# A batched matrix product on one core: the store of group 1 cut into three transfers of 112, 15 and 1 partitions

## The chip, the cores and the metric

The kernel runs on one core of a Trainium2 chip. A core has a matrix engine (TensorE, PE), three other compute engines (VectorE or DVE, ScalarE or ACT, GpSimd or POOL), an engine that issues transfers (SyncE, SP) and 16 DMA engines, which move data between the chip's memory (HBM) and the core's on-chip memory (SBUF, 128 partitions). The metric is the device time of one execution in microseconds. Before the change its median is 132.35 us over 3 runs (132.32 to 132.53).

## The reference

```python
def setup_inputs():
    batch, dim_i, dim_j, dim_k = 32, 256, 512, 384
    return {
        "x": np.random.randn(batch, dim_i, dim_j).astype(np.float32),
        "y": np.random.randn(batch, dim_j, dim_k).astype(np.float32),
    }

def reference(x, y):
    return np.einsum('bij,bjk->bik', x, y).astype(np.float32)
```

There are 32 independent products of a 256 x 512 matrix with a 512 x 384 matrix, in 32-bit floats. x is 16.8 MB, y 25.2 MB and the output 12.6 MB.

## The kernel before, in words

The 32 products are taken in N = 8 groups of Q = 4. For each group the kernel loads a tile of x and a tile of y (two buffers of each, used in turn), casts both to 16 bits on GpSimd, transposes x on VectorE, multiplies on TensorE, copies the results out of PSUM with ScalarE and VectorE, and stores them.

The 128 partitions are four blocks of 32, one for each product of the group. In the output, partition p of group n holds eight consecutive rows of 384 numbers, so one partition's part is 12,288 bytes that lie together both in SBUF and in HBM. The output tile `o_sb` has a slot of its own for each of the 8 groups: a store never makes a later group wait for a buffer.

All transfers are issued by SP, in an order written out by hand. First come the loads of groups 0 and 1, ahead of the main program. Then a loop at the head of SP's part issues the loads of groups 2 to 7 (`load_x` on line 70, `load_y` on line 74), each after a wait for GpSimd's casts of the buffer that it fills. Only then comes a second loop over n from 0 to 7, which issues the stores through `store(n)` (line 97). Ahead of each store stands a wait: for n below 7 until TensorE has finished the first chunk of the second half of group n + 1, which it starts only after group n has been copied out; for n = 7 for the last copies themselves. So in SP's order every load stands ahead of every store.

Each transfer adds 16 to a semaphore when it has landed. The stores share one, `s_out`; nobody looks at it but SP's last instruction (line 112), which waits for 16 x 8 = 128 and takes the count back to zero. That wait is the end of the kernel. POOL clears the other semaphores once SP has issued all stores.

TensorE, VectorE, ScalarE and GpSimd have programs of their own, bound by semaphores; the change touches none of them.

Of the kernel before, what the change touches and what calls it, by code (L numbers as in the profile page):

```python
# [10 lines left out]
P = 128  # L11
Q = 4
NE = 2
STEP = 4
PIECES = 4


@with_exitstack
def kernel(
# [16 lines left out]
    N = B // Q  # L36
    NC = T // STEP
    TY = T // PIECES

# [23 lines left out]
    s_out = nc.alloc_semaphore("s_out")  # L63
# [25 lines left out]
    def chunk_done(n, e, a):  # L89
        return (n * NE + e) * MARKS + (a + 1 if a < NC - 1 else MARKS)  # L90

    sp = nc.sync

    def store(n):
        dst = out[n * Q : (n + 1) * Q].rearrange("g (s f) k -> (g s) f k", s=PQ)
        src = o_sb[:, n].rearrange("p e h k -> p (e h) k")
        sp.dma_start(out=dst, in_=src).then_inc(s_out, 16)

    for n in range(2, N):
        sp.wait_ge(s_cast, NE * (n - 1))  # L100
# [3 lines left out]
    for n in range(N):  # L104
        if n < N - 1:
            sp.wait_ge(s_pe, chunk_done(n + 1, NE - 1, 0))
        else:
            sp.wait_ge(s_act, NE)
            sp.wait_ge(s_dve, NE)
        store(n)  # L110
    sp.sem_inc(s_sp, 1)
    sp.wait_op(s_out, 16 * N, "sem-ge").then_inc(s_out, -16 * N)


    po = nc.gpsimd
    for n in range(N):
# [9 lines left out]
        po.wait_ge(s_y[n], 16)  # L126
        for a in range(PIECES):
            if n:
                po.wait_ge(s_pe, chunk_done(n - 1, NE - 1, (a + 1) * NC // PIECES - 1))
            s = slice(a * TY, (a + 1) * TY)  # L130
            ins = po.tensor_copy(y_r[:, s], y_sb[n % 2][:, s])  # L131
            ins.then_inc(s_yr, 1 if a < PIECES - 1 else 1 + PIECES)
    po.wait_ge(s_sp, 1)
# [124 lines left out]
```

## Time and profile before

| | |
|---|---|
| median of 3 runs | 132.35 us (132.32 to 132.53) |
| the profiled execution | 132.6 us |
| its span | 131.3 us |
| moved by DMA | 54.54 MB (41.94 read from HBM, 12.58 written) |
| DMA transfers | 8 of x (2048 KB each), 8 of y (3072 KB), 8 stores (1536 KB) |
| mean granted TensorE clock | 0.845 |

The profile is of one execution, and its span is the time between the first and the last instruction. Busy times are for each engine over the span; the DMA share is the mean over the core's 16 DMA engines, counted at the start of each packet, which is why a short stretch can show a little over 1. A packet is one piece that one DMA engine moves. In a list of instructions, `L97` is line 97, `SPq` is SP's queue, and "x8" means eight of them. "To landing" is the time from the issue of a transfer until its last byte has been counted on the semaphore. A wait row reads: who waited, at which line, for whom; total us, number of times, longest. A row of the table of stretches reads: from, to, length, busy time (and number of instructions) of PE, PE's weight loads, DVE, ACT and POOL, then the granted clock, the DMA share and the GB/s.

### The profile page before, as it was taken

What the parts mean: (1) busy time and instruction counts of PE and PEld (TensorE: products, weight loads), DVE (VectorE), ACT (ScalarE), POOL (GpSimd) and SP (SyncE); (2) the same over time, 40 slices, a digit from 0 to 9 for tenths busy, and PEclk for the clock granted to TensorE, in tenths of its full rate; (3) what the DMA queues carried; (4) which work ended last, traced back from release to release, by engine and by line L of the source; (5) the groups of instructions that cost most, each with busy time, mean ns of one, the idle gap of its engine ahead of it and who ended that gap; (6) DMA issues with size and microseconds to landing.
All of it is one profiled execution on the core that took longest, in us unless ns stands there. A gap on an engine that the chain in (4) does not pass through costs nothing. (4 is left out here: it accounts for less than half of the span.)

```text
span 131.3 us, 3324 instructions
## 1 busy us (share of the span) xinstructions
PE 64.7 (49%) x1024; PEld 44.1 (34%) x1024; DVE 73.7 (56%) x128; ACT 91.6 (70%) x194; POOL 75.8 (58%) x52
## 2 busy tenths in 40 slices
PE   0000059907980967467278808961994497200000
PEld 0000057606750944235165504441873354100000
DVE  0006005885499499758956993699359859600000
ACT  0400000999599999999997999699969999996000
POOL 0037195589957974997399549857955960000000
PEclk9999999995599599999968997797569869995555
DMA  5999999999999999999999999999999999999994
GB/s 105 419 459 427 417 424 457 427 419 429 457 402 429 437 449 392 439 452 434 402 449 434 424 407 452 442 399 434 449 434 389 429 419 427 438 427 423 431 431 202
DMA packets 3458, 54.54 MB, mean 415 GB/s; under 512 B 384, under 2 KB 384, under 8 KB 384
## 3 DMA queue, kind: packets, MB, share of 16 engines
q1 hardware_dynamic: 3456, 54.53, 97.9%
q14 instruction: 2, 0.02, 0.0%
HBM read 41.94 MB, written 12.58 MB: 415 GB/s over the span
## 5 line engine op out<-in xcount | busy, mean ns | idle before, releaser
L149 ACT COPY o_sb<-o_ps x192 | 90.2, 470 | 24.9 <-PE o_ps L193 22.6
L193 PE MATMUL o_ps<-y_r,xt_sb 32*128 32x384 f16 x1024 | 64.7, 387 | 47.9 <-PEq L190 42.0
L193 PEld LDWEIGHTS o_ps<-y_r,xt_sb 32*128 32x128 f16 x1024 | 44.1, 106 | 68.0 <-issue 58.8
L145 DVE STREAM_TRANSPOSE xt_sb<-x_r 128x256 f32<-128x256 f32 x64 | 38.1, 624 | 38.7 <-PE o_ps L193 27.1
L131 POOL CAST y_r<-y_sb 128x1536 f16<-128x1536 f32 x32 | 45.6, 1467 | 14.0 <-DMA y_sb<-in_y_dram 13.8
L121 POOL CAST x_r<-x_sb 128x2048 f16<-128x2048 f32 x16 | 30.3, 1893 | 17.3 <-DVE o_sb L149 8.8
L149 DVE COPY o_sb<-o_ps 32x384 f32 (+1 forms) x64 | 35.6, 556 | 2.5 <-PE o_ps L193 1.1
L179 ACT ACT_TABLE_LOAD x1 | 1.3, 1283 | 3.7 <-PEq L79 3.7
L242 POOL MEMSET const-float32-0.0<- 128x1 f32 x1 | 0.1, 98 | 0.2 <-issue 0.2
L179 ACT COPY spare<-const-float32-0.0 1x1 f32<-1x1 f32 x1 | 0.2, 190 | 0.0
L242 POOL MEMSET const-bfloat16-1.0<- 128x1 bf16 x1 | 0.1, 101 | 0.0
L242 POOL MEMSET const-uint8-127<- 128x1 uint8 x1 | 0.1, 101 | 0.0
L242 POOL MEMSET const-float32-1.0<- 128x1 f32 x1 | 0.1, 98 | 0.0
## 6 DMA issues: line engine op xcount, KB each, us to landing
y_sb<-in_y_dram SPq DMA_DIRECT2D x8, 3072.0 KB, 16.8
x_sb<-in_x_dram SPq DMA_DIRECT2D x8, 2048.0 KB, 19.0
out_dram<-o_sb SPq DMA_DIRECT2D x8, 1536.0 KB, 24.5
```

Source lines behind the costliest of these rows:

```text
L121: po.tensor_copy(x_r[:, e], x_sb[n % 2][:, e * H : (e + 1) * H]).then_inc(s_cast, 1)
L131: ins = po.tensor_copy(y_r[:, s], y_sb[n % 2][:, s])
L145: v.transpose(xt_w[:, w], words[:, e, w]).then_inc(s_xt, 1)
L149: ins = copy(o_sb[g * PQ : (g + 1) * PQ, n, e, h], o_ps[h * PQ : (h + 1) * PQ, e * Q + g, :K],)
L179: a_.copy(spare, nc.const_aps.tensor(0.0, [1, 1], F32))
L193: return te.add_instruction(mybir.InstMatmult(name=nc.get_next_instruction_name(), start_tensor_calc=start, stop_tensor_calc=stop, tile_si ...
L242: nc = _bacc.Bacc("TRN2", target_bir_lowering=False, num_devices=1)
```

## The change

`store(1)` issues three transfers where it issued one: partitions 0 to 111, then 112 to 126, then 127. The other stores go as one transfer, as before. Each transfer adds 16 to `s_out`, so SP's last wait asks for 16 x 10 = 160.

```diff
+PARTS = [112, 15, 1]
...
     def store(n):
         dst = out[n * Q : (n + 1) * Q].rearrange("g (s f) k -> (g s) f k", s=PQ)
         src = o_sb[:, n].rearrange("p e h k -> p (e h) k")
-        sp.dma_start(out=dst, in_=src).then_inc(s_out, 16)
+        p = 0
+        for w in PARTS if n == 1 else [P]:
+            sp.dma_start(out=dst[p : p + w], in_=src[p : p + w]).then_inc(s_out, 16)
+            p += w
...
-    sp.wait_op(s_out, 16 * N, "sem-ge").then_inc(s_out, -16 * N)
+    sp.wait_op(s_out, 16 * (N + len(PARTS) - 1), "sem-ge").then_inc(s_out, -16 * (N + len(PARTS) - 1))
```

## The prediction

> **What bounds the kernel now.** I read four views, in this order: the head of the page (how busy each engine is), the table of stretches (which resource is full in which stage), the waits of the issuing queue SP, and the packets of the last microseconds. First the page.
>
> ```profile
> span 131.3 us, 3324 instructions
> PE 64.7 (49%) x1024; PEld 44.1 (34%) x1024; DVE 73.7 (56%) x128; ACT 91.6 (70%) x194; POOL 75.8 (58%) x52
> ...
> DMA packets 3458, 54.54 MB, mean 415 GB/s; under 512 B 384, under 2 KB 384, under 8 KB 384
> ...
> q1 hardware_dynamic: 3456, 54.53, 97.9%
> ```
>
> No compute engine is busy for more than 70% of the span; the 16 DMA engines together are busy for 97.9% of it. The packets also tell how a transfer is cut. The kernel issues 24 transfers, and 384 small packets are 24 x 16, so each transfer ends with one small completion write on each of 16 engines. The other 3072 are 24 x 128: one packet per partition row. A row of a store is 1536 KB / 128 = 12 KB, and each engine carries 8 of them.
>
> The table of stretches (length, then busy time of five engines, clock, DMA share, GB/s) says when this holds:
>
> ```profile
> 13.00:26.00 13.00, 8.03 (x127) 6.17 (x128) 4.78 (x8) 2.83 (x7) 7.34 (x5) 1.00 1.01 434
> 26.00:85.00 59.00, 37.27 (x592) 24.61 (x587) 43.83 (x76) 54.03 (x116) 47.40 (x31) 0.86 1.01 431
> 85.00:104.00 19.00, 11.73 (x193) 8.75 (x184) 15.32 (x28) 17.54 (x38) 13.73 (x9) 0.82 0.99 424
> 104.00:128.50 24.50, 7.64 (x127) 4.62 (x125) 7.58 (x13) 15.77 (x34) 3.30 (x3) 0.71 1.01 428
> 128.50:131.30 2.80, 0.00 (x0) 0.00 (x0) 0.00 (x0) 0.00 (x0) 0.00 (x0) 0.50 0.37 158
> ```
>
> The DMA share is full from 13 us to 128.5 us, so what is put on the DMA engines is paid for at the end. The stores run behind the last loads, at 428 GB/s: 1536 KB (1.573 MB) / 428 GB/s = 3.67 us for a store, and with 8 rows for each engine 0.458 us for a row.
>
> Next the stores themselves, in the answer for the output tensor, and SP's own waits:
>
> ```profile
> L97 SPq DMA_DIRECT2D out_dram<-o_sb x8: 332/430/437, 85.1 to 120.2; - x8
> DMA to landing us min/median/max: 11.0/24.5/33.2
> ...
> SPq L97 <- PE o_ps L193: 24.0, 5, 12.2
> SPq L112 <- SPq L112: 10.7, 1, 10.7
> SPq L97 <- ACT o_sb L149: 5.3, 1, 5.3
> ```
>
> A store lands 11.0 to 33.2 us after its issue, though it needs 3.67 us of the engines. The last, issued at 120.2, lands at 120.2 + 11.0 = 131.2, which is the span: three stores lie in the queue even then. SP waits for compute (24.0 and 5.3 us in all) and it costs nothing, since the DMA engines have their backlog. SP's last wait, 10.7 us, is for the stores to land, and it ends the kernel.
>
> Last, the packets from 129 us on, in 40 slices of 0.0575 us. One 12 KB row starting in a slice shows as 12,288 B / 0.0575 us = 214 GB/s, two as 427:
>
> ```profile
> GB/s 641 214 0 427 214 214 427 214 427 0 0 0 0 0 427 214 0 0 0 0 0 0 214 0 0 0 0 0 0 0 0 0 0 0 0 0 0 0 0 0
> DMA packets 33, 0.21 MB, mean 91 GB/s; under 512 B 16, under 2 KB 16, under 8 KB 16
> ...
> 129.70:130.00 0.30, 0.00 (x0) 0.00 (x0) 0.00 (x0) 0.00 (x0) 0.00 (x0) 0.50 0.29 123
> 130.00:130.25 0.25, 0.00 (x0) 0.00 (x0) 0.00 (x0) 0.00 (x0) 0.00 (x0) 0.50 0.00 0
> 130.25:130.30 0.05, 0.00 (x0) 0.00 (x0) 0.00 (x0) 0.00 (x0) 0.00 (x0) 0.50 0.01 0
> 130.30:131.30 1.00, 0.00 (x0) 0.00 (x0) 0.00 (x0) 0.00 (x0) 0.00 (x0) 0.50 0.03 12
> ```
>
> The engines do not end together. Three rows start at about 129.8 to 129.9, and then one engine alone starts a last row at about 130.3. It runs 0.03 x 16 x 1.00 = 0.48 us, the same as a row among sixteen, and lands 0.9 us after it began. Call this the late engine: it has no slack, the next ones have about 0.4 us, the rest up to a microsecond. The rows do not say which of the sixteen it is.
>
> **The change part by part.** It removes one transfer of 128 rows and adds three, of 112, 15 and 1 rows, at the same place in SP's order. The bytes are the same.
>
> Issue on SP: two more issues at 0.332 to 0.437 us each, at most 0.87 us. They stand between store 1 and store 2. Stores 2 to 7 come up to 0.87 us later to a queue that holds 11.0 us of work at its emptiest, and SP itself waits 24.0 us for PE behind them. Cost 0; if the backlog were gone, 0.87 us. The waits in front of the stores are unchanged and no wait is added. The last one asks for 160 in place of 128, with nothing behind it on SP but the end. PE, ACT, DVE and POOL wait for no store, since every group has its own slot of the output tile: 0.
>
> Completion writes: with three transfers an engine makes up to two more. One such write stands alone in the stretch 130.25 to 130.30: 0.01 x 16 x 0.05 = 0.008 us. Two are 0.02 us.
>
> The 112 rows: 112 / 16 = 7 for each engine, if all sixteen share. At the row time that is 3.21 us, and with one more row each it would be the 3.67 of before. No transfer in the trace has fewer than 128 partitions, so whether its rows go at 0.458 us is not shown. In the whole transfer each engine has eight partitions to itself; cut into sevens the shares lie across those eights, and two engines can come to read from the same eight. Bounds: 0, if partitions may be read from any engine at full pace; 7 rows (3.2 us), if every engine shares its path with another all along. The nearest row is the whole transfer, which has 8 row times where this has 7; I take one row, 0.46 us.
>
> The 15 rows: one each for 15 engines, and none for one. The rows are neighbours. Bounds: one row time and no loss, if each engine reads at its own pace as the lone row at 130.3 did; and 15 row times, 6.9 us and so 14 rows lost, if fifteen neighbours come through one path of that same 27 GB/s (428 / 16). The ends are far apart. I take the geometric middle of 1 and 15, four rows in succession, so three rows lost: 1.37 us. It is nearer to the no-loss end, because a lone engine and an engine among sixteen have the same pace and the trace shows no loss in company.
> [...]
>
> The one row: 1/16 row for each engine (0.03 us) if the 12 KB are cut into sixteen; a whole row (0.46) if they stay one packet on the late engine, or if the sixteen parts leave the same partition one after another. I take the row, 0.46, since in every transfer shown a row is one packet.
> [...]
>
> Sum: 1 + 3 + 1 = 5 rows of 0.458 us = 2.29 us, plus 0.02, on an engine without slack. Later stores cannot give it back, for the share is 1.01 until 128.5. The profiled execution took 132.6 us, 1.3 more than its span, and is 0.25 above the median of 132.35. On its span: 133.6. On the median: 132.35 + 2.3 = 134.7. Both ends of all parts: -0.46 (a row less on the late engine) to 22 rows, 10 us.
>
> **The rivals.** *Nothing to see.* Any engine reads any partition at full pace, and the last row is cut sixteen ways or falls to an engine with slack. Then the late engine has 0.02 us of completion writes and 0.03 of the cut row: 132.4. For it: the lone row's pace and the steady 424 to 434 GB/s whatever is moved. Against: all that steadiness is of 128-row transfers.
>
> *Faster: the late engine is the one that the 15 rows leave out.* Then it does 7 rows for store 1 in place of 8, and its last row starts 0.46 us earlier. The engines next to it, 0.4 us ahead, set the end then: 132.35 - 0.4 = 131.95. It decides only if that engine is the late one (1 of 16 if all are alike) and if sharing costs it less than 0.46 us. For it: exactly one late row in the tail. Against: the odds, and any shared path.
>
> *One engine carries the single row whole.* No sharing, but the late engine does 9 rows: 132.35 + 0.46 = 132.8. It decides only if it falls on that engine; on others it is within 0.4 us of slack and vanishes into the first rival.
>
> *Worse sharing.* The 112 rows are dealt out singly, so that sixteen neighbours are read at one time all through: up to the 22 rows of the bounds, 137.2 to 142.4.
>
> **How the numbers follow.** A difference under 0.2% (0.26 us) is about what a measurement of this kernel cannot tell from none. Chances: sharing that costs 0.6 to 4.9 us, with 134.7 as its likeliest, 0.68; worse sharing 0.10; nothing to see 0.12; faster 0.08; one engine alone 0.02. Sharing has most of it because the bounds run from 0 to 22 rows and already the loss of one row on a late engine without slack counts as slower; only at no sharing at all does the time stay. Slower is 0.68 + 0.10 + 0.02 = 0.80, same 0.12, faster 0.08. The range begins just under no change, 132.3, and leaves out the faster case (0.08). It ends at twice the five rows, 4.6 us, plus the 0.25 by which profile and median differ: 137.2. That leaves out the worse sharing (0.10). The slower case alone reaches from 133.0 to 137.2.
>
> **What would show it.** In the changed kernel the packets say how the last row went: 3502 on the hardware queue if it was cut into sixteen (3456 - 144, + 128, + 30, + 32), 3472 if it stayed one (+ 2 in place of + 32). If sharing is right, the GB/s fall under 400 for a few slices where store 1 moves, about 105 to 109 us, while the DMA share stays at 1.0, for the rows take longer; the last store lands over 12 us after its issue; PE, ACT and DVE end where they did. If nothing is shared, the GB/s keep to 424 or more there, and the tail ends again with one lone row near 130.3. If the late engine was left out, the tail has no lone row and ends near 130.8. The prediction is wrong above all if four neighbours go as fast as sixteen strangers, or if the late engine comes to the shared path after the others have gone and pays for none of it.

## The result and the profile after

The changed kernel takes 133.46 us (median of 4 runs, 133.15 to 133.75), the kernel before 132.43 us on the same chip: a ratio of 1.0078, 95% interval [1.0064, 1.0092]. It is slower, by 1.03 us [0.85, 1.22]; 2.3 us were forecast. The direction and the range held, the size did not. A run over 1.5% above the fastest of its kernel counts in no ratio: that leaves out, of the experiments below, two of the eight runs with partitions 0 to 111 alone (134.2 us) and one of the four with all eight stores cut (147.05 us).

From the page of the changed kernel, the lines that answer to those of before:

```profile
span 132.3 us, 3326 instructions
PE 65.3 (49%) x1024; PEld 44.5 (34%) x1024; DVE 73.7 (56%) x128; ACT 91.8 (69%) x194; POOL 75.8 (57%) x52
...
GB/s 114 431 446 439 399 451 416 461 401 471 387 426 436 463 409 421 421 461 424 409 444 431 421 416 451 431 416 426 468 394 416 419 364 424 427 420 431 439 431 141
DMA packets 3474, 54.54 MB, mean 412 GB/s; under 512 B 400, under 2 KB 400, under 8 KB 400
...
q1 hardware_dynamic: 3472, 54.53, 97.6%
...
out_dram<-o_sb SPq DMA_DIRECT2D x7, 1536.0 KB
out_dram<-o_sb SPq DMA_DIRECT2D x1, 1344.0 KB
out_dram<-o_sb SPq DMA_DIRECT2D x1, 180.0 KB
out_dram<-o_sb SPq DMA_DIRECT2D x1, 12.0 KB
```

The compute engines are as busy as before and the bytes are the same. There are 3472 packets on the hardware queue: the last row stayed one packet of 12 KB on one engine, and the small packets, the completion writes, went from 384 to 400 (16 + 15 + 1 for store 1 where there were 16). One slice of the GB/s row, from 105.8 to 109.1 us (number 33), is far below its neighbours: 364. That is where store 1 moves.

The table of stretches of the changed kernel (length, busy times, clock, DMA share, GB/s):

```profile
26.00:85.00 59.00, 38.53 (x596) 24.55 (x595) 44.23 (x77) 54.27 (x116) 47.15 (x30) 0.83 1.01 430
85.00:104.00 19.00, 11.52 (x192) 8.75 (x185) 15.20 (x28) 17.41 (x38) 14.01 (x9) 0.81 1.00 426
104.00:112.00 8.00, 7.05 (x126) 5.27 (x118) 5.08 (x9) 7.79 (x18) 3.01 (x3) 0.81 1.01 396
128.50:132.30 3.80, 0.00 (x0) 0.00 (x0) 0.00 (x0) 0.00 (x0) 0.00 (x0) 0.50 0.41 175
```

and the stretch of store 1 before:

```profile
104.00:112.00 8.00, 7.09 (x122) 4.50 (x124) 5.35 (x9) 7.79 (x17) 3.30 (x3) 0.79 1.01 427
```

Up to 104 us the rates are those of before (430 and 426 against 431 and 424). In the eight microseconds with store 1, the DMA engines are as busy (share 1.01) and move 396 GB/s in place of 427. A share of 31 / 427 of 8 us is lost: 0.58 us, as a mean over the engines. The single packets show how. A row takes 0.460 us in the median in both kernels. Over 0.6 us before there is one row (0.915 us). After there are these twelve, by start, duration and end in ns:

```
104923 1182 106105
104994  915 105909
105688  772 106460
106456  822 107278
106628  818 107446
106996 1672 108668
107062 1531 108593
107145 1993 109138
107289  909 108198
107448 1816 109264
108201 1307 109508
108401 1538 109939
```

One of them is there before as well: in both kernels one row of 0.915 us starts just as an 8 KB packet of the queue `q14 instruction` ends (packet from 104.83 to 105.14 us, row at 105.13 before; packet from 104.69 to 105.00, row at 104.99 after). The other eleven are 9.3 us too long in all, 0.58 us for each of sixteen engines, as much as the GB/s give. Six of them start behind an engine's completion write for the 112 and are rows of the fifteen: 106996, 107062, 107145, 107448, 108201 and 108401. The other five belong to the 112. The longest take four row times (1.82 and 1.99 us).

The trace does not number the engines. But in it nearly every packet starts 3 or 4 ns before another one ends, and by that, and by the count of rows in a store where two end at one time, the packets of one engine can be followed from the last one back. On the engine that ends last in the changed kernel this is store 1 (start, duration in ns):

```
104466  460   seven rows of the 112
104923 1182
106102  460
106558  460
107015  460
107471  460
107928  471
108395    9   completion write
108401 1538   its row of the fifteen
109935    9   completion write
```

From there to the end of its last completion write, at 131.89 us, all its rows take 0.46 us. It lost 0.72 us in the 112 and 1.08 us with the fifteen, and the single row was another engine's: that one started it at 107.72 us and had done with it at 108.18.

SP's waits in the changed kernel:

```profile
SPq L100 <- PE o_ps L197: 22.5, 3, 12.4
SPq L116 <- SPq L116: 11.9, 1, 11.9
```

and the answer for its output tensor (durations of the issues, first and last start):

```profile
L100 SPq DMA_DIRECT2D out_dram<-o_sb x10: 227/392/476, 84.8 to 120.0; - x10
```

The last store is issued at 120.0 us (120.2 before), so compute and SP are not later; only the wait for the stores grew, from 10.7 to 11.9. And the tail from 129 us on (40 slices of 0.0825 us, where one row shows as 149 GB/s):

```profile
GB/s 298 149 1043 149 447 149 0 447 596 0 298 0 149 447 149 298 0 0 298 149 0 149 0 149 149 0 0 0 0 149 0 0 0 0 0 0 0 0 0 0
```

It is longer and thinner. A lone last row starts at about 131.4 us; before, it started at about 130.3.

### The profile page after: what moved, and what is told of

It is laid out like the page before. It is cut to its first block, busy times and chain, and to the rows that moved or that the text cites. A ratio compares the mean times of both kernels' runs of the same rounds, so it can differ in the third digit from the quotient of the medians.

```text
span 132.3 us, 3326 instructions
## 1 busy us (share of the span) xinstructions
PE 65.3 (49%) x1024; PEld 44.5 (34%) x1024; DVE 73.7 (56%) x128; ACT 91.8 (69%) x194; POOL 75.8 (57%) x52
## 3 DMA queue, kind: packets, MB, share of 16 engines
q1 hardware_dynamic: 3472, 54.53, 97.6%
```

## The experiments

Theory S: rows of neighbouring partitions share a path to SBUF, so transfers that reach few partitions at one time, or divide the rows otherwise than the whole store does, make engines wait for one another. Rival U: the uneven share, since one engine has nine rows of store 1 (seven of the 112, one of the fifteen, and the single row from 107.72 to 108.18 us). Rival C: each further transfer costs by itself. The gains and losses below are the ratio times the median of the kernel before on the same chip (132.57 us for the first four kernels, 132.38 for the four that size the terms and cut all stores, 132.37 for three more, 132.52 for the last).

**112 and 16 rows.** Every engine has eight rows again.

```diff
-PARTS = [112, 15, 1]
+PARTS = [112, 16]
```

> Store 1 as 112 and 16 rows; no engine has a ninth row and none is left out. Theory S (rows of neighbouring partitions share a path to SBUF): the loss of the changed kernel, 1.0 us, stays: 133.2 to 133.7 us. Rival U (the loss is the uneven share: one engine carries nine rows, as the single row went as one packet): the loss goes, 132.3 to 132.6 us.

Measured: ratio 1.0066 [1.0044, 1.0088], 0.87 us slower [0.58, 1.17]. The loss stays without any ninth row, so U falls as the cause of the whole loss.

**Without the last row.**

```diff
-PARTS = [112, 15, 1]
+PARTS = [112, 15]
```

> Store 1 as 112 and 15 rows; partition 127 of group 1 is not stored (left out). S: what the single row costs goes and the rest stays, 133.0 to 133.5 us. U: no engine has a ninth row, back to 132.2 to 132.5 us.

Measured: 133.45 us, ratio 1.0062 [1.0039, 1.0084], 0.82 us slower. Against the 1.03 us of the changed kernel the single row costs 0.2 us, between about -0.1 and 0.6 by the two intervals: it cannot be told from nothing, and its forecast 0.46 is not excluded by this run alone.

**Eight transfers of 16, neighbours against spread.** The same transfers, sizes, packets and shares; only which partitions go together differs.

```diff
-PARTS = [112, 15, 1]
+PARTS = [16] * 8
```

> Store 1 as eight transfers of 16 neighbouring partitions, one row for each engine in each; all 128 rows go. S: each of them loses between 0.4 us (a mean over the engines as in the changed kernel) and 1.4 us (four rows in succession in place of one), 3 to 11 us in all: 135.5 to 143 us. U: all engines have eight rows, 132.4 to 132.7 us. Rival C (each further transfer costs, whatever its rows): seven more transfers at 0.3 to 0.5 us each, 134.5 to 136 us, and the same with the rows spread.

```diff
-PARTS = [112, 15, 1]
+PARTS = [16] * 8
...
-        p = 0
-        for w in PARTS if n == 1 else [P]:
-            sp.dma_start(out=dst[p : p + w], in_=src[p : p + w]).then_inc(s_out, 16)
-            p += w
+        m = len(PARTS) if n == 1 else 1
+        for i in range(m):
+            sp.dma_start(out=dst[i::m], in_=src[i::m]).then_inc(s_out, 16)
```

> Store 1 as eight transfers of 16 partitions with a step of 8 (0, 8, ... 120; then 1, 9, ...), one row for each engine in each. The same transfers, packets and shares as with eight neighbours; only which partitions go together differs. S: less than half the loss of the eight neighbours, 133 to 137 us. C: the same time as the eight neighbours. U: 132.4 to 132.7 us.

Measured: neighbours 1.0381 [1.0351, 1.0410], 5.1 us slower; spread 1.0110 [1.0091, 1.0129], 1.5 us slower. On both pages the queue has 3568 packets; the neighbours' line:

```profile
q1 hardware_dynamic: 3568, 54.53, 95.9%
```

The stretch of store 1 of the neighbours:

```profile
104.00:112.00 8.00, 6.29 (x123) 3.74 (x127) 5.15 (x9) 7.21 (x16) 3.86 (x3) 1.00 1.00 290
```

and of the spread rows:

```profile
104.00:112.00 8.00, 6.98 (x127) 5.06 (x120) 4.96 (x9) 7.56 (x17) 3.26 (x3) 0.85 1.01 357
```

With the same 3568 packets and a full DMA share, 290 GB/s against 357. Of the rows, 26 take over 1.2 us with neighbours, and one where they are spread; there most long rows take 0.6 to 1.0, two row times. So C falls as the main cause: two kernels with the same number of transfers differ by 3.6 us. Which rows move together decides, as S has it. Two things stay open. The 1.5 us of the spread rows may hold a cost for each transfer: their long rows are 1.2 us too long for each engine in the mean, and no run separates the rest. And rows that are neighbours in SBUF are neighbours in the output in HBM too, in every run here; so that they meet on the SBUF side, and not in HBM, is assumed in S and not shown.

**112 rows alone, 16 alone, 16 spread alone, and the upper 112 alone.** These were to size the terms; each leaves the other rows of group 1 out.

```diff
-PARTS = [112, 15, 1]
+PARTS = [112]
```

> Store 1 sends partitions 0 to 111 alone; 112 to 127 of group 1 are not stored (left out). Each engine has seven rows in place of eight. If the 112 rows lose nothing: 132.5 - 0.46 = 132.0 us. If they lose one row on the engine that ends last, as the prediction sized it: 132.5. If they carry the whole loss of the changed kernel: 133.0.

```diff
-PARTS = [112, 15, 1]
+PARTS = [16]
...
+        if n == 1:
+            dst, src = dst[112:], src[112:]
```

> Store 1 sends partitions 112 to 127 alone; 0 to 111 of group 1 are not stored (left out). One row for each engine in place of eight: 132.5 - 7 x 0.458 = 129.3 us without a loss. With three rows lost on the engine that ends last, as the prediction sized the fifteen: 130.7. If engines with slack take most of the loss: 129.4 to 130.2.

```diff
-PARTS = [112, 15, 1]
+PARTS = [16]
...
+        if n == 1:
+            dst, src = dst[::8], src[::8]
```

> Store 1 sends sixteen partitions with a step of 8 (0, 8, ... 120) alone; the other 112 of group 1 are not stored (left out). The same bytes and packets as with the neighbours 112 to 127. If neighbours share a path and these less so: 129.2 to 129.6 us, and less than with the neighbours. If the loss belongs to any short transfer: the same time as with the neighbours.

The last one came after the others, to see whether the loss of the 112 belongs to sevens as such:

```diff
-PARTS = [112, 15, 1]
+PARTS = [112]
...
+        if n == 1:
+            dst, src = dst[16:], src[16:]
```

> Store 1 sends partitions 16 to 127 alone; 0 to 15 of group 1 are not stored (left out). Seven rows for each engine, as with partitions 0 to 111 alone. If sevens that lie across the usual shares are the largest term of the changed kernel: 132.6 to 133.2 us, as with 0 to 111. If what 0 to 111 lost was an accident of those partitions or of those runs: 131.9 to 132.2 us, seven rows without a loss.

Measured, partitions 0 to 111 alone: ratio 1.0027 [1.0002, 1.0053], which is 132.74 us, where seven rows without a loss give 131.92: a loss of about 0.8 us [0.5, 1.2]. It varies from run to run: the eight runs go from 132.06 to 134.19 us, and their median, 133.09, would give 1.2.

Partitions 16 to 127 alone: ratio 0.9960 [0.9947, 0.9974], which is 131.99 us, where seven rows without a loss give 132.06: no loss, and all five runs lie within 0.12 us. They ran on another chip than those of 0 to 111, each against the kernel before on its own chip. The stretches of store 1, of 0 to 111:

```profile
104.00:112.00 8.00, 7.09 (x125) 4.57 (x120) 5.24 (x9) 7.79 (x18) 3.16 (x3) 0.79 1.01 416
```

and of 16 to 127:

```profile
104.00:112.00 8.00, 7.03 (x120) 5.30 (x122) 5.40 (x10) 7.80 (x17) 3.34 (x3) 0.80 1.01 425
```

Nine rows over 0.6 us with 0 to 111 (3.7 us too long in all), two with 16 to 127 (0.6 us); one of each is the row behind the instruction packet. So sevens as such need not lose, and no run tells by what rule these did. With 0 to 111 the mean loss over the engines is (427 - 416) / 427 x 8 us = 0.2 us and the end pays 0.8: the engine that ends last, followed as above, has three of the long rows, 1.48 us too long.

The 16 neighbours alone: 0.9770 [0.9754, 0.9785], which is 129.34 us, where one row without a loss gives 129.17: a loss of 0.16 us [-0.05, 0.36]. The 16 spread rows: 0.9768 [0.9751, 0.9784]; the end shows no difference to the neighbours, against what I expected of S. The rows differ a little: four over 0.6 us with neighbours (the longest 0.89), one with the spread (0.90). One of each is again the row behind the instruction packet, so three long rows are left with neighbours, 0.8 us too long in all, and none with the spread.

**64 and 64 rows.** Nothing is short and every engine has eight rows.

```diff
-PARTS = [112, 15, 1]
+PARTS = [64, 64]
```

> Store 1 as two transfers of 64 partitions, four rows for each engine in each; every engine has its eight rows and nothing is short. If neighbours share a path and 64 of them reach half of the paths, every engine meets another all along: four more rows in each transfer at most, 8 x 0.458 = 3.7 us; 135.0 to 136.2 us. If only short transfers lose: 132.4 to 132.7. If any cut of a store costs about what the changed kernel's costs: 133.4.

```profile
104.00:112.00 8.00, 8.00 (x126) 6.60 (x118) 4.79 (x8) 6.94 (x16) 3.07 (x3) 0.65 1.01 336
```

Measured: 1.0163 [1.0136, 1.0189], 2.2 us slower. It lies between the cases that I named: more than if only short transfers lost or any cut cost the same, less than a full meeting all along (3.7). Of 128 rows 58 take over 0.6 us, 30 of them 0.8 to 1.0, two row times. Two large halves lose twice what the changed kernel loses, so a transfer need not be small to cost.

**All eight stores cut.**

```diff
-        for w in PARTS if n == 1 else [P]:
+        for w in PARTS:
...
-    sp.wait_op(s_out, 16 * (N + len(PARTS) - 1), "sem-ge").then_inc(s_out, -16 * (N + len(PARTS) - 1))
+    sp.wait_op(s_out, 16 * N * len(PARTS), "sem-ge").then_inc(s_out, -16 * N * len(PARTS))
```

> All eight stores go as 112, 15 and 1 partitions. If each split costs what the one costs (1.0 us): 132.5 + 8 = 140.5 us. If the first one draws the engines apart, so that later ones meet less: 134 to 138. If the loss is hidden in later stores by engines that wait anyway: under 134.

Measured: ratio 1.0910 [1.0889, 1.0930], 12.0 us slower: 1.5 us for each cut, above all three cases. That engines once drawn apart meet less is wrong here; why a cut among cuts costs more than one among whole stores was not tried.

**The last store cut, and the opposite order.**

```diff
-        for w in PARTS if n == 1 else [P]:
+        for w in PARTS if n == N - 1 else [P]:
```

> The same cut into 112, 15 and 1, but of the last store and not of store 1. If a loss stays to the end because nothing behind it has slack, the place does not matter: 133.2 to 133.7 us, as the changed kernel. If the engines could give something back in the six stores behind store 1, the last store costs more: 133.8 to 135.0.

```diff
-PARTS = [112, 15, 1]
+PARTS = [1, 15, 112]
```

> Store 1 as 1, 15 and 112 partitions: the same sizes in the opposite order (partition 0; 1 to 15; 16 to 127). If the loss depends on the sizes alone: 133.2 to 133.7 us, as the changed kernel. If it depends on how far apart the engines are when they reach the narrow transfers: another time, by 0.3 us or more.

Measured: the last store cut, 1.0044 [1.0013, 1.0075], 0.6 us slower [0.2, 1.0], with runs from 132.25 to 134.06. It costs not more than store 1 cut, so there is no sign that the six stores behind store 1 give anything back. In the opposite order, 1.0068 [1.0041, 1.0095], 0.9 us: the same as the changed kernel within the interval. Yet here the 112 are partitions 16 to 127, which alone lose nothing. So the pieces' losses are not a fixed price for each that adds up, unless partitions 1 to 15 cost far more than 112 to 127 do alone (0.16 us), which was not measured.

## Why the prediction was right and wrong

*The bound.* Right. The DMA share is full wherever it was (1.00 or 1.01 in each stretch from 13 to 128.5 us), compute and SP end no later, and what store 1 loses comes out at the end.

*Two more issues and the completion writes at nothing.* Right: the last store is issued at 120.0, and a completion write takes 9 ns.

*The packets.* 3472, the second of the two counts: the single row stayed whole. Of the 400 small packets 23 x 16 belong to the other transfers; 32 are left, 16, 15 and 1 for the three pieces, and they start between 106.81 and 109.94 us.

*That neighbours share a path.* Right in that rows of neighbouring partitions slow each other when they move together, shown by eight transfers of 16 with 290 GB/s as neighbours and 357 when spread, and by rows of four row times (1.82 and 1.99 us) in the changed kernel itself. That the path is on the SBUF side is not shown.

*The sum of 1 + 3 + 1 rows on an engine without slack.* This step failed. The engine that ends last in the changed kernel lost 0.72 + 1.08 = 1.80 us, where the sum has 2.29, and it did have slack: without these 1.80 us it would have ended at 131.89 - 1.80 = 130.09 us, and in the kernel before the last engine ended at 130.77. So 0.7 us of its loss went into slack, and 1.1 came out at the end (the two spans differ by 1.0). The late engine of the kernel before can be followed too: its rows take 0.47 to 0.56 us from 103 to 113 us. In the changed kernel the engine with such rows took 0.545 us for its row of the fifteen and ended at 130.75, where it ended before. It paid for none of the sharing, and another engine came in behind it. This is so in the two profiled executions; other runs were not followed. Term by term:

- The 15 rows were put at three rows, 1.37 us. Rows of four row times do occur, but six of the fifteen rows were long, and the one on the engine that ended last was 1.08 us too long. By the times the term is smaller still: 16 neighbours alone cost the end 0.16 us [-0.05, 0.36], and 112 and 16 cost 0.87 where the 112 alone cost about 0.8. I had taken the price of a row on a crowded path as the price at the end.
- The single row was put at 0.46 us. It went whole to one engine, which had done with it at 108.18 us; the engine that ended last finished its row of the fifteen at 109.94. So in the profiled execution it cost the end nothing.
- The 112 rows were put at one row, 0.46, an estimate that took sevens to lie across eights; which partitions an engine takes, no view shows. They took 0.72 on the engine that ended last, and partitions 0 to 111 alone cost about 0.8 [0.5, 1.2], partitions 16 to 127 alone nothing. The reason that I gave would hold for both, so it is not enough; why the lower ones lose is open.

Under all three terms lies the same error: I priced each part on its own and let the late engine pay for all of them. The eleven long rows are 0.58 us in the mean over sixteen engines, and the end paid 1.03. The end paid more than this mean in three others too: 1.5 against 1.2 us with eight spread transfers, 2.2 against 1.7 with two halves, 5.1 against 2.7 with eight neighbours. How much more does not follow from the pieces alone: 112 and 16, 112 and 15, and the opposite order all cost 0.8 to 0.9 us, though their pieces alone cost from 0 to 0.8. (In the changed kernel's own order the two measured pieces, 0.8 and 0.16, do come near the 1.03.) The prediction itself named as a sign of being wrong that the late engine may pay for none of the shared path, and then priced the sum as if it paid for all of it.

*Later stores cannot give it back.* Held within the interval: the cut of the last store costs no more, and on the engine that ends last every row behind store 1 takes 0.46 us.

*The rivals.* "Nothing to see" and "faster" are outside the interval. "One engine carries the single row whole" describes what the packets did, but its 132.8 is below the interval too, and with 112 and 16 the loss is the same. "Worse sharing" did not come: only five rows of the 112 were long.

What stays open: which of the sixteen the engine that ends last is, and whether it is the same in other runs; whether the rows meet at SBUF or in HBM; by what rule partitions 0 to 111 lose and 16 to 127 do not; why a cut among cuts costs 1.5 us; and why the kernel with the last store cut varies between 132.25 and 134.06 us, where the kernel before stays within 0.6 us beside it. Taking a piece's conflicts away by dealing its rows to chosen engines was not tried.

## What to carry to other kernels

On a full DMA queue, keep a store whole over all 128 partitions: cut across the partitions it moved the same bytes with the same engines here and still lost, more with two halves (2.2 us) than with 112, 15 and 1 (1.0 us). If a transfer must be cut, judge a piece by which rows its engines move at the same moment, not by its size alone: pieces of 16 moved at 290 GB/s as neighbours and at 357 when spread. To price a loss on parallel engines, do not add up the worst of each part on one engine: here that gave 2.3 us, the mean over the engines by the GB/s of the stretch 0.58, and the end paid 1.03. Look for the engine that takes the loss and for its slack: here it lost 1.8 us and had 0.7 to spare.

## What the runs showed of the hardware

- A full DMA share did not tell the pace: from 104 to 112 us it is 1.00 at 290 GB/s with eight transfers of neighbours, and 1.01 at 427 in the kernel before. With neighbours 26 rows took over 1.2 us.
- A row of 12 KB takes 0.460 us in the median in the kernel before and in the changed one, and up to 1.99 us in the changed one, 2.49 with eight neighbours.
- Sixteen engines on one queue did not keep step: in the kernel before, the last store's last rows start between 128.7 and 130.3 us. There one engine alone starts its last row 0.4 us after the next ones; it is one whose rows took 0.47 to 0.56 us from 103 to 113 us, and why is open.
- One row beside the instruction queue's 8 KB packet was long: in the kernel before and in the changed one a row of 0.915 us in place of 0.46 starts as that packet ends (at 105.14 and 105.00 us).
- 112 partitions from 0 on lost about 0.8 us (0.5 to 1.2, and very unevenly, 132.06 to 134.19 us from run to run), 112 from 16 on nothing, though both are seven rows for each engine and one transfer.
